# Attention values in seven products with sums of x's quarters, the second head pair's score steps seven slots later, and four branch gates ahead of their gate products

## The chip, the cores and the metric

The kernel runs on one core of one Trainium2 chip. The metric is the device time of one execution in microseconds (us). Before the change the median of three timed runs is 757.07 us (756.86 to 757.54). Engines are named as in the profile: PE is TensorE's matrix multiply, PEld its weight load, DVE is VectorE, ACT is ScalarE, POOL is GpSimd, SP is SyncE, which here only issues DMAs.

## What is computed

One decoder block over 512 tokens of width 1024, in float32. One input projection feeds two token mixers whose outputs are gated, added, projected, normalised, and followed by a feed-forward block. Cut to what matters here:

```python
p = einsum('btd,de->bte', h, w_in) + b_in
a_u, a_v, q, k, v, r, a_low, g_a, g_b = split(p)
y_a = spatial_gating(a_u, a_v, ...)
log_f = log_sigmoid(a_low @ gla_w_gate2 + gla_b_gate) / 16
o = gla_chunked(q, k, v, log_f)          # 4 heads, key 128, value 256
o = o * rsqrt(mean(o**2) + eps)
y_b = o * gla_norm_g * silu(r)
m = sigmoid(g_a) * y_a + sigmoid(g_b) * y_b
h = layer_norm(alpha * h + m @ w_out)
h = layer_norm(alpha * h + square(relu(h @ w_ff1)) @ w_ff2)
```

The change concerns `v` (512 tokens x 1024 values, contracted over 1024), the head pair 1 of `gla_chunked` (heads 2 and 3), and the products `r` and `g_b`.

## The kernel before, in words

**Numbers in two parts.** Every large product is made in three matmul passes. An operand is split into a high part, a rounded copy that ACT writes (CAST, line 88), and a low part, the rest, that DVE writes (TENSOR_TENSOR, line 89). The passes are high x high, high x low and low x high. x lives as `xh`, `xl`; a weight chunk of 128x1024 numbers becomes `wh`, `wl`.

**The weight stream.** `_stream` (line 1109) lists the chunks in order of use. `load_to` issues their DMAs from SP into a ring of three raw buffers, `sum_to` makes sums of chunks where the list asks for them (DVE, line 128), and `split_to` splits them up to seven chunks ahead of PE (`W_BUFS`). A raw buffer is loaded again only when DVE has read it; a `wh`/`wl` buffer is written again only when PE has used it.

**Slots.** PE's order is the order of the program. Each group of 24 matmuls of 128x512 (one bank of PSUM) is a slot; a group is either `row_unit` with tokens as rows (line 218) or `col_job` with tokens as columns (line 691). `at(n, f, phase=...)` puts side work into slot n, and `pump` calls it after that slot's matmuls: first phase MM (other matmuls), then MAIN, then the splits of the next weight chunk, then LATE. DVE, ACT and POOL run in the order in which these calls issue their instructions, strictly one after the other.

**The stages before.** Slots 0 to 7: gating values (`ps`, line 218). 8 to 15: `u`. 16 to 19: q and k of pair 1 (`qk1`). 20 to 27: attention values, two row units of four groups, 8 weight chunks, 192 matmuls; DVE adds the bias row and writes `bufB` (line 785). 28 to 35: `ga`. Then `branch` four times: two slots `r`, two slots `gb`. From 52 on `m @ w_out`, then the feed-forward stage, whose second half already uses seven products for eight (lines 934 to 984, a Strassen-Winograd scheme with three running accumulators).

**Pair 1's score steps.** `plan_pair` (line 589) spreads them: gates (`gates_b`, running sums `cum`), `inter_a`, `inter_e`, `inter_b` (`kd`, `QI`), transposes `pt`, three levels of decayed scores (`level_diff`, `level_prep`, scores `sc`, line 519, masked into `AT` by three DVE copies each, line 532), the diagonal (`diag_a` to `diag_c`, `sd`, line 493), then `chunk_out` (`po`) with the running state `S`. Before, the levels stand in slots 21 to 32, the diagonal's scores in 34 and 35, and `chunk_out` in 36 to 39.

**PSUM.** Eight banks: four for the groups (pool `ps_m`, rotating), two that all score tiles share as one buffer (`ps_s`, tag `sc`, used by `pz`, `sc`, `sd` and by the transposes `yt` in `r_take`, line 797), two of `ps_a`.

**`r_take` and `gb_take`.** After an `r` group PE transposes the attention output into `yt`, ACT makes silu, DVE multiplies (line 801). After a `gb` group ACT makes the sigmoid and DVE multiplies and adds into `AT_` (lines 816, 817); from the second branch on `mh`, `ml` are split at once.

## Time and profile before

| | |
|---|---|
| median of three runs | 757.07 us |
| the profiled execution itself | 757.19 us |
| its span, first to last instruction | 755.4 us |
| PE busy | 746.2 us, 99% of the span |
| DVE busy | 473.8 us, 63% |
| ACT busy | 343.6 us, 45% |
| POOL busy | 29.8 us, 4% |
| DMA moved | 85.14 MB, mean 113 GB/s |
| granted TensorE clock, mean | 0.998 |

The time of an execution is 1.8 us more than its span. A row of the timeline shows start, duration, engine, line, operation, output and inputs; brackets hold the idle time before it and what ended it. A matmul's listed duration (389 ns) overlaps its neighbours; what one costs is the distance between starts.

The same stretch in slices (busy us of each engine) shows DVE at 5.51 of 11 us in the last two `qk1` groups (150 to 161 us) and 8.65 of 11 us in the first two value groups (161 to 172 us).

### The profile page before, as it was taken

How to read it: one execution, taken by the hardware profiler on the slowest of the kernel's cores; microseconds unless marked ns; L12 is line 12 of the kernel's file. 1: busy time of each engine (PE TensorE's matmuls, PEld its weight loads, DVE VectorE, ACT ScalarE, POOL GpSimd, SP SyncE). 2: the span in 40 equal slices, each digit the busy share in tenths (PEclk: the TensorE clock that was granted, in tenths of full speed). 3: DMA queues.
4: the chain of work that ended last, by engine and by line, in shares of the span. 5: the costliest groups of instructions: out<-in, count | busy, mean ns of one | idle time of the engine just before them, and what ended most of it. 6: DMA issues, size and time to landing. Idle time of an engine off the chain costs nothing.

```text
span 755.4 us, 8781 instructions
## 1 busy us (share of the span) xinstructions
PE 746.2 (99%) x3498; PEld 626.0 (83%) x3498; DVE 473.8 (63%) x592; ACT 343.6 (45%) x449; POOL 29.8 (4%) x60
## 2 busy tenths in 40 slices
PE   9999999999999999999999999999999999999996
PEld 7878888888888888888888988888888888888885
DVE  7478876676575554435458533777667856687655
ACT  7375744363254735444222544444444554455300
POOL 1000000000000102000002000000000000000001
PEclk9999999999999999999999999999999999999999
DMA  8533322222042132432240324145331734135111
GB/s 341 203 134 125 132 82 80 84 84 84 31 145 77 56 126 84 170 109 85 98 152 31 109 72 147 49 134 201 111 112 34 244 100 152 56 125 196 43 56 56
DMA packets 25464, 85.14 MB, mean 113 GB/s; under 512 B 3088, under 2 KB 3344, under 8 KB 25424
## 3 DMA queue, kind: packets, MB, share of 16 engines
q1 hardware_dynamic: 25280, 84.33, 32.3%
q8 instruction: 27, 0.44, 0.2%
q10 hardware_dynamic: 144, 0.26, 0.1%
q14 instruction: 13, 0.11, 0.0%
HBM read 82.48 MB, written 2.10 MB: 112 GB/s over the span
## 4 chain that ended last, share of the span: by engine, by line
PE 96%; issue 1%; DVE 1%; DMA 1%; POOL 0%; DVEq 0%; POOLq 0%
PE f L691 22%; PE ps L218 17%; PE mx L974 9%; PE f L1074 6%; PE gb L691 6%; PE r L691 6%; PE ga L691 6%; PE u L691 6%; PE mv L974 4%; PE qk L691 3%; PE first L275 3%; PE m L974 2%; PE sc L519 2%; PE pm L744 1%; PE po L553 1%
## 5 line engine op out<-in xcount | busy, mean ns | idle before, releaser
L89 DVE TENSOR_TENSOR wl<-raw,wh 128x1024 fp32r<-128x1024 f32 x141 | 171.1, 1222 | 114.4 <-ACT wh L88 112.6
L88 ACT CAST wh<-raw 128x1024 fp32r<-128x1024 f32 x141 | 145.7, 1044 | 48.7 <-PE ps L218 23.7
L691 PE MATMUL f<-xh,wh 128*128 128x512 f32 (+1 forms) x288 | 105.4, 366 | 0.0
L691 PE MATMUL f<-xl,wh 128*128 128x512 f32 (+1 forms) x288 | 105.3, 365 | 0.0
L691 PE MATMUL f<-xh,wl 128*128 128x512 f32 (+1 forms) x288 | 105.2, 365 | 0.0
L691 PEld LDWEIGHTS f<-xl,wh 128*128 128x128 f32 x288 | 54.3, 189 | 8.8
L691 PEld LDWEIGHTS f<-xh,wl 128*128 128x128 f32 x288 | 54.3, 189 | 8.7
L691 PEld LDWEIGHTS f<-xh,wh 128*128 128x128 f32 x288 | 54.3, 189 | 8.7
L914 ACT ACTIVATE F<-f 128x512 f32<-128x512 f32 (+1 forms) x28 | 15.0, 537 | 80.2 <-PE f L691 79.1
L218 PE MATMUL ps<-wh,xh 128*128 128x512 f32 x128 | 50.4, 394 | 0.0
L218 PE MATMUL ps<-wh,xl 128*128 128x512 f32 x128 | 49.8, 389 | 0.0
L218 PE MATMUL ps<-wl,xh 128*128 128x512 f32 x128 | 49.8, 389 | 0.0
L974 PE MATMUL mx<-wh,oh 128*128 128x512 f32 x96 | 37.3, 389 | 0.0
L974 PE MATMUL mx<-wl,oh 128*128 128x512 f32 x96 | 37.3, 389 | 0.0
L974 PE MATMUL mx<-wh,ol 128*128 128x512 f32 x96 | 37.3, 389 | 0.0
L128 DVE TENSOR_TENSOR raw<-raw,raw 128x1024 f32<-128x1024 f32 x24 | 29.2, 1218 | 2.6 <-DMA raw<-in_w_all 2.6
L218 PEld LDWEIGHTS ps<-wh,xl 128*128 128x128 f32 x128 | 24.0, 188 | 5.0
L218 PEld LDWEIGHTS ps<-wl,xh 128*128 128x128 f32 x128 | 24.0, 188 | 4.9
L218 PEld LDWEIGHTS ps<-wh,xh 128*128 128x128 f32 x128 | 24.0, 188 | 4.8
L691 PE MATMUL u<-xh,wh 128*128 128x512 f32 x64 | 25.9, 405 | 0.0
L691 PE MATMUL ga<-xh,wh 128*128 128x512 f32 x64 | 25.9, 404 | 0.0
L88 ACT CAST oh<-d 128x1024 fp32r<-128x1024 f32 x12 | 12.6, 1051 | 29.1 <-DVE d L947 29.1
(242 smaller groups left out, 1557.4 us busy)
## 6 DMA issues: line engine op xcount, KB each, us to landing
raw<-in_w_all SPq DMA_DIRECT2D x136, 512.0 KB, 3.4
bufB<-in_head SPq DMA_DIRECT2D x4, 512.0 KB, 8.0
xr<-in_x SPq DMA_DIRECT2D x8, 256.0 KB, 3.5
out<-bufA SPq DMA_DIRECT2D x8, 256.0 KB, 2.0
bufA<-in_head SPq DMA_DIRECT2D x3, 512.0 KB, 5.6
brow<-in_b_in SPq DMA_DIRECT2D x4, 256.0 KB, 6.2
g<-in_ln_g SPq DMA_DIRECT2D x2, 512.0 KB, 5.9
b<-in_ln_b SPq DMA_DIRECT2D x2, 512.0 KB, 5.5
```

What stands on the lines that cost most here:

```text
L88: nc.scalar.copy(hi, src)
L89: nc.vector.tensor_tensor(lo, src, hi.bitcast(F32), op=ALU.subtract)
L128: nc.vector.tensor_tensor(raw, x_, y_, op=ALU.subtract)
L218: nc.tensor.matmul(ps, s_, m_, start=(k == 0 and i == 0), stop=(k == KT - 1 and i == 2))
L275: nc.tensor.matmul(first[e], s_, m_[:, k, :], start=(k == 0 and i == 0), stop=(k == KT - 1 and i == 2))
L519: nc.tensor.matmul(sc[:, c, 0:192], pr.kt[:, jc * P : (jc + 1) * P], pr.qt[:, jc, :], start=True, stop=True)
L553: nc.tensor.matmul(po, pr.AT[:, j, c, :], vs, start=True, stop=(c == 0))
L691: nc.tensor.matmul(ps, s_, m_, start=(k == 0 and i == 0), stop=(k == KT - 1 and i == 2))
L744: nc.tensor.matmul(pm[:, c, :], bufB[:, c, gs], wst[:, g, :], start=True, stop=True)
L914: nc.scalar.activation(dst, ps, AF.Relu)
L974: nc.tensor.matmul(ps, s_, m_, start=(begins and k == 0 and i == 0), stop=(k == 3 and i == 2), skip_group_check=True,)
L1074: nc.tensor.matmul(ps, s_, m_, start=(f == 0 and i == 0), stop=(f == 7 and i == 2))
```

## The change

**Values in seven products.** The values are split in two halves of tokens and columns, and contracted over two halves of 512. x's quarters are summed into four combinations, the weights' quarters into four combinations, and seven products of 24 matmuls each (2 banks of 12) take the place of eight groups. The order is 1, 2, 5, 6, 3, 7, 4. Products 1, 6, 7, 4 run on in one pair of banks, 5 and 3 in another; after each half product DVE adds the bank (running sum included) into a quarter of `bufB`. `value_bank` gives products 2, 5 and 3 the same two banks.

What that takes: 14 weight splits for 8, eight sums of weight chunks on DVE, a second load of x's transposed quarters from `head` into `bufB` (eight DMAs of 256 KB), four sums of quarters (`x_sums`, in slot 19, MAIN), and four splits of the sums (`x_parts`).

**Slots.** The value stage has seven slots (20 to 26). Pair 1's steps move: `gates_b` stays in 18, `inter_a` goes from 19 to 26, the levels from 21..32 to 28..39, the diagonal's scores to 41 and 42, `chunk_out` to 43..46. Thus the levels' later part and the diagonal now stand in the stage of `r` and `gb`.

**Branch order.** `r0 r1 gb0 gb1 r2 r3 gb2 gb3` as before, then `gb4 gb5 gb6 gb7` with their sigmoids kept in `bufB`, then `r4 r5 r6 r7`, each followed by its multiplication, its addition and its split. The four splits of `mh`, `ml` for e below 4 come together before `r4`.

The core of the diff (names and bodies moved without a change left out):

```diff
-    ps_m = pool(ctx, "ps_m", bufs=4, space=PSUM)
+    ps_m = pool(ctx, "ps_m", bufs=1, space=PSUM)
...
+    def bank(name, i=None):
+        if i is None:
+            i = turns[0]
+        turns[0] = (i + 1) % 4
+        return ps_m.tile([P, 512], F32, name=name, tag=f"ps{i}")
...
+    RAW_AT = {(1, 1): (0, 0), (0, 0): (1, 1), (0, 1): (0, 1), (1, 0): (1, 0)}
+    def accumulators(m, name, of):
+        if m in (1, 6, 7, 4):
+            if m == 1:
+                sums["x"] = [of(f"mx{name}_{t}", "x", t) for t in range(2)]
+            return sums["x"], m == 1
+        if m in (5, 3):
+            if m == 5:
+                sums["v"] = [of(f"mv{name}_{t}", "v", t) for t in range(2)]
+            return sums["v"], m == 5
+        return [of(f"m{name}_{t}", "m", t) for t in range(2)], True
...
+    def operands_begin():
+        sgu.close()
+        vgp = pool(vgs, "vgp", side="left")
+        vgp.tile([P, 120], F32, name="pad_v")
+        for (i, j), (a, b) in RAW_AT.items():
+            for k in range(2):
+                k0 = 4 * j + 2 * k
+                nc.sync.dma_start(xq(a, b)[:, k], head[:, k0 : k0 + 2, 256 * i : 256 * i + 256])
+        return vgp
...
-    S_VG, S_GA = 20, 28
-    S_R, S_O = 36, 52
+    S_VG, S_GA = 20, 27
+    S_R, S_O = 35, 51
...
-    plan_pair(pr1, (18, 19, 20, 21), ((21, 23, 24, 25), (25, 27, 28, 29), (29, 30, 31, 32)), 32)
+    plan_pair(pr1, (18, 26, 27, 28), ((28, 30, 31, 32), (32, 34, 35, 36), (36, 37, 38, 39)), 39)
...
+    def x_sums():
+        for o, a, b, op_ in (
+            ((0, 0), (1, 0), (0, 0), ALU.add),
+            ((1, 0), (1, 1), (1, 0), ALU.subtract),
+            ((1, 1), (0, 0), (1, 1), ALU.subtract),
+            ((0, 1), (0, 1), (1, 1), ALU.subtract),
+        ):
+            nc.vector.tensor_tensor(quarter(bufB, *o), quarter(bufB, *a), quarter(bufB, *b), op=op_)
+    at(S_VG - 1, x_sums)
+    at(S_VG - 1, lambda: x_parts(5), phase=LATE)
...
-    for half in range(2):
-        row_unit(xh, xl, copy_take(half, bias_row(C_VG + half * 512)))
+    def value_bank(name, kind, t):
+        return bank(name, (b0 + t + 2 * (kind != "x")) % 4)
+    def value_take(m, t, ps):
+        dst = quarter(bufB, *GOES[m])[:, t, :]
+        nc.vector.tensor_add(dst, brs[GOES[m][1]] if m in NEW else dst, ps)
+    for n, m in enumerate(ORDER):
+        if m == 2:
+            x_parts(6)
+        elif m in (6, 3):
+            x_parts({6: 3, 3: 7}[m])
...
+        product_of(f"v{m}", m, ops, value_take, value_bank, W_BUFS - n // 2)
+        pump(MM, MAIN)
+        pump(LATE)
...
+    for e0 in (0, 2):
         t1 = {e: temp(f"t1_{e}", "brow") for e in (e0, e0 + 1)}
         for e in t1:
             col_job(f"r{e}", r_take(e, t1[e]))
         for e in t1:
-            col_job(f"gb{e}", gb_take(e, t1[e]))
+            col_job(f"gb{e}", gb_take(e, temp(f"gb{e}"), t1[e]))
+    gate = {e: bufB[:, e - 4, 0:512] for e in range(4, KT)}
+    for e in gate:
+        col_job(f"gb{e}", gb_take(e, gate[e]))
...
+        def parts_take(ps, e=e, t1=t1, take=take):
+            take(ps)
+            onto(e, gate[e], t1)
+            split(mh[:, e, :], ml[:, e, :], AT_[:, e, :])
...
+    out += [operand(-1, m, h) for m in ORDER for h in range(2)] + plain(28, n)
```

What moves on the engines shows at three places. First DVE at the end of `qk1` and the start of the values. Before (`wl` are weight splits, `ps_24` the banks of the first value groups):

```order
L381 SCALAR_TENSOR_TENSOR cum1_1297<-ones_97,lf1_1242 128x128 x8
L89 TENSOR_TENSOR wl29_1308<-raw29_1157,wh29_1307 128x1024
L391 TENSOR_TENSOR kd1_1339<-cum1_1297 128x1024
L89 TENSOR_TENSOR wl30_1342<-raw30_1207,wh30_1341 128x1024
L785 TENSOR_TENSOR bufB_92<-ps_24_0_1352,brow_1350 128x512
L401 TENSOR_TENSOR QI1_1268<-QI1_1268,q1_1162 128x1024
```

And DVE of the changed kernel from the row after the running sums on (`raw24<-raw30,raw24` is a sum of weight chunks; `bufB<-bufB` x4 are `x_sums`; `xl5`, `xl6` are splits of x's sums; `mxv1_0` is the first bank of product 1, `mv2_0` that of product 2):

```order
L128 TENSOR_TENSOR raw24_863<-raw30_1162,raw24_863 128x1024
L89 TENSOR_TENSOR wl29_1317<-raw25_865,wh29_1316 128x1024
L857 TENSOR_TENSOR bufB_92<-bufB_92 128x2x512 x4
L128 TENSOR_TENSOR raw25_865<-raw31_1164,raw25_865 128x1024
L89 TENSOR_TENSOR wl30_1354<-raw24_863,wh30_1353 128x1024
L89 TENSOR_TENSOR xl5_1361<-bufB_92,xh5_1360 128x1024
L886 TENSOR_TENSOR bufB_92<-brow_1364,mxv1_0_1368 128x512
L89 TENSOR_TENSOR wl31_1390<-raw25_865,wh31_1389 128x1024
L89 TENSOR_TENSOR wl32_1402<-raw30_1162,wh32_1401 128x1024
L886 TENSOR_TENSOR bufB_92<-brow_1364,mxv1_1_1369 128x512
L89 TENSOR_TENSOR xl6_1407<-bufB_92,xh6_1406 128x1024
L886 TENSOR_TENSOR bufB_92<-bufB_92,mv2_0_1410 128x512
```

Pair 1's `kd` and `QI` are gone from there, and fourteen sums, splits and additions stand between the running sums and the read of product 2's first bank, which is the bank that product 5 takes next.

Second, PE at the end of `r0`. Before:

```order
L691 MATMUL r0_2100<-xh_89,wl40_1763 128x512
L799 MATMUL yt0_2125<-ident_93,bufB_92 128x128 x4
L553 MATMUL po2_0_2132<-bufB_92,AT1_1266 128x256
L557 MATMUL po2_0_2132<-bufB_92,KD1_1269 128x256
L553 MATMUL po3_0_2135<-bufB_92,AT1_1266 128x256
L557 MATMUL po3_0_2135<-bufB_92,KD1_1269 128x256
L691 MATMUL r1_2160<-xh_89,wh41_1809 128x512
```

And in the changed kernel:

```order
L767 MATMUL r0_2083<-xh_89,wh46_1800 128x512
L767 MATMUL r0_2083<-xl_90,wh46_1800 128x512
L767 MATMUL r0_2083<-xh_89,wl46_1801 128x512
L910 MATMUL yt0_2108<-ident_93,bufB_92 128x128 x4
L583 MATMUL sc1_1_0_2115<-qt1_1_1979,kt1_1_2000 128x192 x4
L767 MATMUL r1_2129<-xh_89,wh47_1804 128x512
```

A score tile now follows the transposes at once; both lie in the one buffer `sc`. The same holds after `r1` and `r2`.

Third, DVE around the second head's diagonal. Before (`dr1_1` are its products, `sd1_0` the first head's scores, `dt1_1` the low part that PE's `sd1_1` needs):

```order
L471 TENSOR_TENSOR dr1_1_2005<-q1_1162,k1_1163 128x512
L711 TENSOR_TENSOR bufA_91<-bufA_91,ga5_1976 128x512
L479 TENSOR_TENSOR dr1_1_2005<-dr1_1_2005,q1_1162 128x256
L480 TENSOR_TENSOR dr1_1_2005<-dr1_1_2005,k1_1163 128x256
L89 TENSOR_TENSOR wl45_2048<-raw45_1874,wh45_2047 128x1024
L500 COPY_PREDICATED AT1_1266<-masks_279,sd1_0_2038 128x512
L505 COPY_PREDICATED AT1_1266<-masks_279,sd1_0_2038 128x256
L484 TENSOR_TENSOR dt1_1_2043<-dr1_1_2005,dt1_1_2043 128x768
```

And now:

```order
L535 TENSOR_TENSOR dr1_1_2359<-q1_1169,k1_1170 128x512
L924 TENSOR_TENSOR t1_2_2265<-t1_2_2265,gb2_2362 128x512
L925 TENSOR_TENSOR bufA_91<-bufA_91,t1_2_2265 128x512
L543 TENSOR_TENSOR dr1_1_2359<-dr1_1_2359,q1_1169 128x256
L544 TENSOR_TENSOR dr1_1_2359<-dr1_1_2359,k1_1170 128x256
L89 TENSOR_TENSOR wl59_2401<-raw59_2260,wh59_2400 128x1024
L564 COPY_PREDICATED AT1_1639<-masks_282,sd1_0_2391 128x512
L569 COPY_PREDICATED AT1_1639<-masks_282,sd1_0_2391 128x256
L548 TENSOR_TENSOR dt1_1_2396<-dr1_1_2359,dt1_1_2396 128x768
```

The multiplication with the group `ga5`, which was already a slot old, is replaced by two steps that need the sigmoid of the group `gb2` just made.

## The prediction

> **What bounds the kernel now.** I read the page's head and the summary of its chain first.

> ```profile
> span 755.4 us, 8781 instructions
> PE 746.2 (99%) x3498; PEld 626.0 (83%) x3498; DVE 473.8 (63%) x592; ACT 343.6 (45%) x449; POOL 29.8 (4%) x60
> PE 96%; issue 1%; DVE 1%; DMA 1%; POOL 0%; DVEq 0%; POOLq 0%
> ```

> PE is busy for 99% of the span and carries 96% of the chain. So a matmul less is time less, and every wait that the change puts before a matmul is time more. DVE is at 63% on average, which says nothing about the stage that changes. There I need rows in order of time; the chain, merged, shows PE from the last `qk1` groups to the end of the values.

> ```profile
> 150.31 10.90 PE qk L691 x48
> 161.21 10.88 PE ps L218 x48
> 172.10 0.87 PE pt L408 x8
> 172.97 16.34 PE ps L218 x72
> 189.31 1.30 PE sc L519 x8
> 190.61 5.45 PE ps L218 x24
> 196.06 1.30 PE sc L519 x8
> 197.36 10.89 PE ps L218 x48
> ```

> The reader is to see no gap: PE goes from 150.31 to 208.25 without a wait. A matmul of 128x512 costs 10.88 / 48 = 0.227 us, a slot of 24 costs 5.44 us, a half product of 12 costs 2.72 us.

> **Term 1: matmuls removed.** The values take 7 x 24 = 168 matmuls for 192. 24 x 0.227 = **-5.44 us**. All were on the path. The `pt` and `sc` rows between them (0.87 + 1.30 + 1.30) are moved, not removed.

> **Term 2: PE waits for DVE inside the values.** Product 5 takes the two banks of product 2, directly after it, so its first matmul waits until DVE has added product 2's first bank (`mv2_0`). When DVE gets there is a sum over its queue. Its rows of before:

> ```profile
> 158.31 1.23 DVE L89 TENSOR_TENSOR wl<-raw,wh 128x1024 fp32r<-128x1024 f32 x1 [3.55 <-ACT wh L88]
> 159.45 1.22 DVE L377 TENSOR_TENSOR lf<-lf,ab 128x1024 f32<-128x1024 f32 x1
> 160.71 2.63 DVE L381 TENSOR_TENSOR_SCAN cum<-ones,lf 128x128 f32<-128x128 f32 x8
> 163.25 1.20 DVE L89 TENSOR_TENSOR wl<-raw,wh 128x1024 fp32r<-128x1024 f32 x1
> 164.37 1.22 DVE L391 TENSOR_TENSOR kd<-cum 128x1024 f32<-128x1024 f32 x1
> 165.51 1.22 DVE L89 TENSOR_TENSOR wl<-raw,wh 128x1024 fp32r<-128x1024 f32 x1
> 166.69 0.69 DVE L785 TENSOR_TENSOR bufB<-ps,brow 128x512 f32<-128x512 f32 x1
> 167.30 1.22 DVE L401 TENSOR_TENSOR QI<-QI,q 128x1024 f32<-128x1024 f32 x1
> ```

> DVE starts at 158.31 because ACT's `wh` came only then (its bracket says so), behind pair 1's gates, which don't move. From there one 1024-wide instruction follows the other at 1.14 us (164.37 to 165.51), a 512-wide addition takes 0.61 (166.69 to 167.30). The added chunk sums in slots 16 and 17 fit into the 3.55 us of idle time and I cost them at nothing. The mean of one (the second number after the bar) is from the groups by shape:

> ```profile
> L128 DVE TENSOR_TENSOR raw<-raw,raw 128x1024 f32<-128x1024 f32 x24 | 29.2, 1218 | 2.6 <-DMA raw<-in_w_all 2.6
> L816 DVE TENSOR_TENSOR gb<-gb,t 128x512 f32<-128x512 f32 x8 | 5.5, 692 | 25.0 <-ACT gb L815 25.0
> ```
> ```profile
> L88 ACT CAST wh<-raw 128x1024 fp32r<-128x1024 f32 x141 | 145.7, 1044 | 48.7 <-PE ps L218 23.7 <-DMA raw<-in_w_all 11.0 <-PE mx L974 9.9
> ```

> `x_sums` are the same operation as line 128 on as many numbers, so 1.22 each, 1.14 in a row.

> From the end of the scans at 163.25 the changed queue holds ahead of `mv2_0`: a chunk sum, `wl29`, four `x_sums`, a chunk sum, `wl30`, `xl5`, `wl31`, `wl32`, `xl6`, which is 12 x 1.14 = 13.7 us, and two additions, 1.2 us. So `mv2_0` starts at 178.15 and ends at 178.85. ACT's casts keep ahead: 1.04 us each, one for each of DVE's splits and none for its sums. PE, starting the values at 161.21, is through products 1 and 2 at 161.21 + 48 x 0.227 = 172.1. **PE waits 6.8 us.**

> The second half of product 5 waits for `mv2_1`. Ahead of that stand two chunk sums and two splits: 4 x 1.14 + 0.6 + 0.7, so it ends at 184.05. PE, on again at 178.9, is through the first half at 181.6: **2.4 us more.** After that DVE has per product of 5.44 us at most three or four 1024-wide instructions and two additions, 4.6 to 5.8 us; adding the queue up row by row, products 6, 3, 7 and 4 find their operands about 2 us early or more (the closest: product 4's first bank, free at 201.1, wanted at 203.1). Sum of term 2: **+9.2 us.** The values end at 161.2 + 38.1 + 9.2 = 208.5, with the 3.5 us of `pt` and `sc` still to come.

> How sure is 9.2? If every 1024-wide instruction took 1.1, the first wait is 0.5 smaller. If x's second load came late, it grows: eight loads of 256 KB, most of them released when `mix` has read `bufB` at about 150 us, are needed at 165.5. Loads of that size (the last number is the median to landing):

> ```profile
> xr<-in_x SPq DMA_DIRECT2D x8, 256.0 KB, 3.5
> ```

> So I cost them at nothing. Bounds for term 2: 8.2 to 11.

> **Term 3: transposes and scores share one buffer.** In slots 35, 36 and 39, a score tile stands right behind the transposes `yt` of the same group and needs their buffer. It waits until DVE's multiplication has read `yt`, which waits for ACT's silu. How long that takes, three views of before show for `r0`: the chain, ACT's and DVE's rows.

> ```profile
> 273.28 0.44 PE yt L799 x4
> ```
> ```profile
> 273.32 0.69 ACT L800 ACTIVATE t<-r,cols_sb 128x512 f32<-128x512 f32 x1 [3.83 <-PE r L691]
> ```
> ```profile
> 274.04 0.75 DVE L801 SCALAR_TENSOR_TENSOR t<-yt,cols_sb,t 128x512 f32<-128x512 f32 x1 [2.67 <-ACT t L800]
> ```

> Transposes done at 273.72, buffer free at 274.79 plus about 0.05: 1.1 us. Before, `po` followed there, which lies elsewhere. Three times: **+3.3 us**. It can't be hidden, since nothing stands between on PE. Bounds: 2.5 (0.85 each, if ACT and PE overlap better) to 4.5 (DVE is late once).

> **Term 4: the second head's diagonal.** `sd1_1` needs DVE's low part `dt1_1` and the buffer of `sd1_0`. Before, this was already the one place here where PE waited:

> ```profile
> 253.12 0.43 PE po L553 x2
> ...
> 260.36 0.70 PE sd L493 x4
> 261.06 5.47 PE ga L691 x24
> ...
> 266.57 0.47 DVE dt L484
> ```
> ```profile
> 259.93 1.28 ACT L710 ACT_TABLE_LOAD   x1
> 261.22 0.69 ACT L710 ACTIVATE ga<-ga,cols_sb 128x512 f32<-128x512 f32 x1
> 261.81 0.82 ACT L481 CAST dt<-dr 128x768 fp32r<-128x768 f32 x1
> ```
> ```profile
> 265.52 0.73 DVE L505 COPY_PREDICATED AT<-masks,sd 128x256 f32<-128x256 uint32 x1
> 266.05 0.98 DVE L484 TENSOR_TENSOR dt<-dr,dt 128x768 fp32r<-128x768 f32 x1
> ```

> From the end of the group at 260.36, ACT's sigmoid came 0.86 late (behind the table load), and `dt` ended at 267.03, 6.67 us after the group; the next group and `sd` took 6.2, and PE waited 0.57 us. Two things lengthen it now. The slot before is 5.88 us (0.44 + 5.44) where it was 7.24 (253.12 to 260.36, with four `po` pairs in it), while ACT's and DVE's chain through it stays about 8.1 us (253.12 to 261.22): the sigmoid comes 2.2 late, 1.3 more. And between that sigmoid and the cast of `dt` DVE now has a multiplication and an addition (1.4 us, line 816's 692 ns twice) and the two 256-wide products, which stood ahead of it before (between half of 0.69 and 0.69 each; I take 0.45, 0.9 us): 2.3 more. So `dt1_1` ends 6.67 + 1.3 + 2.3 = 10.3 us after the group, PE is there after about 6.4, and waits 3.9 where it waited 0.57: **+3.3 us**. The other scores of the stage lose at most 0.2 us each, **+0.3 us** together. Bounds: -0.6 (the wait goes altogether) to 4.5.

> **Nothing else.** The `gb` groups ahead of `r`: their order costs no matmul. At the end the chain from `r7` is silu, three DVE steps, cast and split, 0.69 + 0.75 + 0.69 + 0.69, a cast of half the 1.04 us width (at most 1.04) and 0.69 = 4.6 us, and the last part of `mh` is needed 0.44 + 21 x 0.227 = 5.2 us after `r7`: hidden, by a margin of 0.6 us. SP's loads of the next chunks have one slot per chunk after the values.

> **Sum.** -5.44 + 9.2 + 3.3 + 3.3 + 0.3 = +10.7. On the profiled execution's 757.19 us (span 755.4, 1.8 around it, 0.1 above the median): **767.8 us.**

> **The clock.** PE's granted clock falls when PE is idle; the slices at the end show it.

> ```profile
> 748.00:749.00 1.00, 0.41 (x4) 0.20 (x2) 0.52 (x2) 0.00 (x0) 0.00 (x0) 1.00 0.00 0
> 751.00:752.00 1.00, 0.00 (x0) 0.00 (x0) 1.00 (x3) 0.00 (x0) 0.00 (x0) 1.00 0.00 0
> 752.00:753.00 1.00, 0.00 (x0) 0.00 (x0) 0.43 (x1) 0.00 (x0) 0.00 (x0) 0.68 0.36 143
> ```

> The last matmul ends at 748.4, and the clock (third last column) is halved at about 752.4, 4.0 us later. A wait of 6.8 us therefore ends at half clock, one of 3.9 may. At half clock a half product takes 5.44 for 2.72 us. After the first wait that lies within the 2.4 us of the second one, all but 0.3.

> [...]

> **The rivals.**
> [...]
> - *The values alone.* DVE's mean load of 63% leaves room behind the values; if term 4 doesn't come and the buffer waits are short, -5.44 + 9.2 + 2.5 - 0.6: **762.9**. Against it: the order of the rows that term 4 adds up.
> - *Faster.* If the read of product 2's bank is not behind the sums, or DVE is ahead by more than I count, no wait stays and the 24 matmuls and the old wait of 0.57 go: **751.2**. It is decided by whether DVE gets from `wl28` to the end of `mv2_0` in 13.8 us (158.3 to 172.1); my sum is 20.5. For it: DVE's idle time of 3.55 us just before, and a mean load of 63%. Against: that idle time is a wait for ACT which stays.
> - *No change.* The first wait alone, the others hidden: -5.44 + 6.8 - 0.6, **758.0**. Against it: what follows it on DVE, four instructions of 1.14 us in a half product of 2.72.

> **How the numbers follow.** Forecast 0.58; clock on top 0.14; values alone 0.15; faster 0.08; no change 0.05. Slower by over 0.2% (1.5 us, about what a measurement can tell from no change) 0.87, within 0.05, faster 0.08. The range runs from 760.5 (term 2 at 8.2 and terms 3 and 4 at their low ends give 761.9; 1.4 less if the second wait of term 2 is more than halved) to 772 (the clock's upper end).

> **What the changed profile would show.** Right: PE idle before the first matmul of the fifth value bank, put down to DVE's addition, near 6.8 us, and a shorter one of 2 to 2.5 at the next bank; three waits near 1.1 us of `sc` for the multiplication with `yt`; one of 3 to 4 us at `sd`; a clock below 1.00 near 179 us. Wrong: no wait in the values, or waits for DMA there (x's second load), or DVE idle between `cum` and `mv2_0`.

## The result, and the profile after

| | before | after |
|---|---|---|
| median | 757.15 us (756.86 to 757.54, 5 runs) | 772.98 us (772.60 to 774.44, 5 runs) |
| the profiled execution | 757.19 us | 773.63 us |
| its span | 755.4 us | 771.9 us |
| granted TensorE clock, mean | 0.998 | 0.988 |

The ratio is 1.0211 (95% interval 1.0200 to 1.0222): slower, as forecast, and 1.0 us above the range's upper end. One of the four executions of `three`, below, took 1527.99 us, twice as long as its others, for a reason that nothing on record shows; its median here is that of the other three. The head of the page after, and the shares of its chain:

```profile
PE 747.3 (97%) x3474; PEld 624.6 (81%) x3474; DVE 502.9 (65%) x620; ACT 352.1 (46%) x458; POOL 29.9 (4%) x60
PE 88%; DVE 6%; ACT 3%; issue 2%; DMA 1%; POOL 0%; DVEq 0%; ACTq 0%; POOLq 0%
```

PE has 24 matmuls less and yet 1.1 us more busy time, since some of them ran at half clock. Its share of the chain fell from 96% to 88%; DVE, which had 1%, has 6%: PE now waits for it. What PE waits for between 150 and 400 us (in total, times, longest):

```profile
PE mvv L372 <- DVE bufB L886: 7.6, 2, 7.4
PE sd L557 <- DVE AT L569: 4.4, 1, 4.4
PE sc L583 <- DVE t L912: 3.4, 3, 1.1
```

`mvv` are the two banks of products 5 and 3, `AT` the masked scores, `t` the product with `yt`. These are the three places that the prediction named. To see what they cost, take PE's timeline at three borders: the first matmul of the values (161.05 before, 161.00 after), of `ga0`, and of the stage after the last branch. The two borders of before, and of after:

```profile
208.09 0.39 PE L691 MATMUL ga<-xh,wh 128*128 128x512 f32 x1
...
367.32 0.39 PE L218 MATMUL ps<-wh,mh 128*128 128x512 f32 x1
```
```profile
209.18 0.39 PE L767 MATMUL ga<-xh,wh 128*128 128x512 f32 x1
...
383.05 0.48 PE L227 MATMUL ps<-wh,mh 128*128 128x512 f32 x1
```

At the last border the change is 15.7 us behind. From there to the last matmul (748.4 before, 764.7 after) another 0.6 us comes in small pieces, in which the profile shows no wait of PE. The values took 48.2 us instead of 47.0, although 3.5 us of `pt` and `sc` have left them. Like for like they cost 4.7 us more; the other 11 us arise between the borders, in the stage of `r` and `gb` (the `ga` stage before it runs without a wait).

The clock also shows in the windows (stretch, its length, busy time of PE, PEld, DVE, ACT, POOL, then the granted clock third from the end):

```profile
176.00:177.00 1.00, 0.00 (x0) 0.00 (x0) 1.00 (x2) 0.00 (x0) 0.00 (x0) 0.89 0.00 0
183.00:184.00 1.00, 1.00 (x5) 0.77 (x3) 1.00 (x2) 0.00 (x0) 0.00 (x0) 0.70 0.32 94
...
323.00:324.00 1.00, 0.00 (x0) 0.00 (x0) 0.89 (x1) 1.00 (x3) 0.00 (x0) 0.77 0.00 0
330.00:331.00 1.00, 1.00 (x5) 0.77 (x5) 0.37 (x1) 0.00 (x0) 0.00 (x0) 0.81 0.75 213
```

A clock of 0.5 for a part of a slice gives the moment: it halves at 176.78, is back at 183.60, halves at 323.54 and is back at 330.38. The second half-speed stretch hits `sd1_1` and `gb4`, with nothing to hide it.

### The profile page after: what moved, and what is told of

Its sections match the earlier page's. It is cut to its first block, busy times and chain, and to the rows that moved or that the text cites. A ratio compares the mean times of both kernels' runs of the same rounds, so it can differ in the third digit from the quotient of the medians.

```text
span 771.9 us, 8815 instructions
## 1 busy us (share of the span) xinstructions
PE 747.3 (97%) x3474; PEld 624.6 (81%) x3474; DVE 502.9 (65%) x620; ACT 352.1 (46%) x458; POOL 29.9 (4%) x60
## 4 chain that ended last, share of the span: by engine, by line
PE 88%; DVE 6%; ACT 3%; issue 2%; DMA 1%; POOL 0%; DVEq 0%; ACTq 0%; POOLq 0%
PE f L767 22%; PE ps L227 11%; PE mx L372 8%; PE r L767 6%; PE ga L767 6%; PE u L767 6%; PE f L1154 5%; PE gb L767 4%; PE mv L372 4%; PE first L286 3%; PE sc L583 2%; PE m L372 2%; PE mxv L372 2%; DVE wl L89 2%; PE qk L767 1%
## 5 line engine op out<-in xcount | busy, mean ns | idle before, releaser
L89 DVE TENSOR_TENSOR wl<-raw,wh 128x1024 fp32r<-128x1024 f32 x147 | 178.1, 1222 | 123.8 <-ACT wh L88 122.6
L88 ACT CAST wh<-raw 128x1024 fp32r<-128x1024 f32 x147 | 151.6, 1044 | 62.6 <-DVE raw L128 19.1
L128 DVE TENSOR_TENSOR raw<-raw,raw 128x1024 f32<-128x1024 f32 x32 | 39.0, 1218 | 2.6 <-DMA raw<-in_w_all 2.5
L767 PE MATMUL gb<-xh,wh 128*128 128x512 f32 x64 | 26.3, 412 | 0.0
L88 ACT CAST oh<-d 128x1024 fp32r<-128x1024 f32 x12 | 12.6, 1051 | 29.1 <-DVE d L1057 29.1
L767 PE MATMUL r<-xh,wh 128*128 128x512 f32 x64 | 25.8, 404 | 0.0
L767 PE MATMUL gb<-xh,wl 128*128 128x512 f32 x64 | 25.5, 399 | 0.0
L767 PE MATMUL gb<-xl,wh 128*128 128x512 f32 x64 | 25.4, 397 | 0.0
L227 PE MATMUL ps<-wh,mh 128*128 128x512 f32 x64 | 25.2, 393 | 0.0
L227 PE MATMUL ps<-wh,xh 128*128 128x512 f32 x64 | 25.2, 393 | 0.0
## 6 DMA issues: line engine op xcount, KB each, us to landing
bufB<-in_head SPq DMA_DIRECT2D x8, 256.0 KB, 4.3
xr<-in_x SPq DMA_DIRECT2D x8, 256.0 KB, 3.8
out<-bufA SPq DMA_DIRECT2D x8, 256.0 KB, 2.0
brow<-in_b_in SPq DMA_DIRECT2D x4, 256.0 KB, 6.5
```

What stands on the lines that cost most here:

```text
L88: nc.scalar.copy(hi, src)
L89: nc.vector.tensor_tensor(lo, src, hi.bitcast(F32), op=ALU.subtract)
L128: nc.vector.tensor_tensor(raw, x_, y_, op=ALU.subtract)
L227: nc.tensor.matmul(ps, s_, m_, start=(k == 0 and i == 0), stop=(k == KT - 1 and i == 2))
L767: nc.tensor.matmul(ps, s_, m_, start=(k == 0 and i == 0), stop=(k == KT - 1 and i == 2))
```

## The experiments

All kernels are the change with the edit shown; times are medians of timed runs, beside 757.1 to 757.2 for before on the same chips.

### What holds the values back

**own_banks**: product 2 away from product 5's banks.

```diff
     def value_bank(name, kind, t):
+        if kind == "m":
+            return ps_a.tile([P, 512], F32, name=name, tag="aux")
```

> Product 2 gets two PSUM banks of its own (the free pair of ps_a), so product 5 no longer waits for product 2's additions. Theory 'DVE queue' (DVE's work in the values is longer than PE's, the bank only shows it): PE starts product 5 at about 174 us, after a wait of about 2 us instead of 7.4, but stands again for about 5 us before product 3, whose x parts DVE still ends near 190 us; gain 2.5 us at most, about 770.5 us, less if that second wait halves the clock. Rival 'shared bank' (the wait comes from the buffer alone): the 7.4 us wait shrinks to about 2 and nothing takes its place, 5.5 us faster, about 767.5 us.

Measured: 772.12 us (ratio 1.0195, 1.0180 to 1.0210), 0.9 faster. PE's waits of this kernel in the values:

```profile
PE mvv L372 <- DVE xl L89: 4.6, 2, 3.2
PE mvv L372 <- DVE bufB L888: 0.6, 1, 0.6
```

The wait of 7.4 us is gone and 5.2 us have come in its place, 3.2 of them before product 3 and followed by half clock (0.50 from 189 to 190 us). The shared bank was where the wait showed, not what it was made of: DVE's queue sets the pace.

**pool_sums**: the sums of x's quarters on the idle engine.

```diff
-            nc.vector.tensor_tensor(quarter(bufB, *o), ...)
+            nc.gpsimd.tensor_tensor(quarter(bufB, *o), ...)
```

> The four sums of x's quarters (5.0 us on DVE) go to POOL, which is idle there; nothing else changes. Theory 'DVE queue': everything behind them on DVE comes 5 us earlier, so PE's wait before product 5 falls from 7.4 to about 2.4 us, the next one stays near 2.3, and the clock stays at 1.00 there: about 5 us faster, 768 us. Rival: POOL takes longer for the sums than DVE, or slows DVE beside it, and the x parts come as late as before: no gain, 772 to 774 us. (No row of the trace has such a sum on POOL.)

Measured: 773.42 us (1.0210, 1.0193 to 1.0227), no gain. One sum on POOL and two instructions of DVE beside it:

```profile
160.96 3.26 POOL L857 TENSOR_TENSOR bufB<-bufB 128x1024 f32<-128x1024 f32 x1
```
```profile
158.56 3.40 DVE L89 TENSOR_TENSOR wl<-raw,wh 128x1024 fp32r<-128x1024 f32 x1 [2.41 <-ACT wh L88]
161.88 3.41 DVE L441 TENSOR_TENSOR lf<-lf,ab 128x1024 f32<-128x1024 f32 x1
```

In the change, with POOL idle there, these two instructions take 1.23 and 1.22 us; beside POOL's sums they take 3.40 and 3.41: 2 x 2.2 us lost there, of the 5.0 that left the queue.

**no_sums**: the same load taken off DVE without giving it to POOL.

```diff
-    at(S_VG - 1, x_sums)
```

> Leaves out the four sums of x's quarters (the products take the quarters as they are), so that DVE has 5.0 us less ahead of product 5 and POOL nothing more. Theory 'DVE queue': PE's wait before product 5 falls from 7.4 to about 2.4, the next is about 2.3, the clock stays at 1.00: 5 us faster than the change, 768 us. Rival: something else than DVE's work holds the bank (x's load, ACT): 772 us or more.

Measured: 769.89 us (1.0168, 1.0152 to 1.0184), 3.1 faster; the waits are 2.6 and 2.2 us, as expected. The values took 45.0 us for 48.2. The rest of the 5 us went to the clock, which fell at 180.41, behind the two waits, for one stretch of 3.41 us with nothing to hide it. What DVE has queued, and not x's load or ACT, makes the first wait.

**three**, **three_pool**, **three_no_sums**, **three_no_dve**: `own_banks`, `own_yt` and `late_onto` (both below) together, then with the sums on POOL, left out, and with the sums of weight quarters left out too.

```diff
-                if less:
+                if less and i > 40:
```

> own_banks, own_yt and late_onto together. Theory 'separate terms': their gains add up, 0.9 + 2.2 + 3.7 = 6.8 us, 766.2 us; the waits of the scores for the rows yt and the fall of the clock at sd1_1 go, the waits of product 5 and product 3 for x's parts stay. Rival: the waits share DVE's queue, and what one frees is late at the next: 768 us or more.

> The same three, and the sums of x's quarters on POOL. Theory 'DVE queue': the 5 us that leave DVE take away the waits of 1.4, 0.6 and 3.2 us for x's parts and the half clock behind the last of them: about 6 us below 'three', near 760 us, and still slower than before. Rival: POOL is late with the sums: like 'three', 766 us.

> 'three' without the four sums of x's quarters. Theory 'DVE queue': product 3's x parts come 5 us earlier, near 185 us, PE waits about 2.5 us there instead of 1.4 + 0.6 + 3.2 in three places: 4 to 6 us below 'three', about 761 us. Rival: as 'three', 766 us.

> 'three' without the four sums of x's quarters and without the eight sums of weight quarters (the products take quarters as they are; 14 us less on DVE). Theory: no wait stays in the values, which end about 8.5 us earlier than in 'three': about 758 us. So even with DVE's added work taken out, the 5.4 us of fewer matmuls are about eaten by what the displaced score steps still cost. Rival: the values still wait for loads or ACT: 762 us or more.

Measured: 766.03 (1.0115, 1.0099 to 1.0132), 765.76 (1.0118, 1.0099 to 1.0137), 759.53 (1.0029, 1.0019 to 1.0039) and 758.14 us (1.0015, 1.0005 to 1.0024). The gains of the three add up (7.0 us for 6.8). POOL helps no more here than alone: that expectation was 6 us off, as it left out that the two DVE instructions take 3.40 and 3.41 us beside POOL's sums here too. Without the sums of x's quarters 6.5 us go, a little more than the 4 to 6 expected: the values take 40.0 us for 46.4, since the waits shrink from 5.2 to 1.3 us and no half clock follows them (189 to 190 us at 1.00, in `three` at 0.50). In the profiled execution (758.25 us) the clock didn't fall at `sd1_1` either. That is not so in most: of nine executions three took 757.9 to 758.3 us at a mean clock of 0.997, and six 759.5 to 760.6 at 0.994 or 0.995. Without any sums no wait is left in the values, as the waits of `three_no_dve` between 150 and 400 us show, all of them:

```profile
PE sd L557 <- DVE AT L569: 2.0, 1, 2.0
PE sc L583 <- DVE kt L528: 1.3, 1, 1.3
```

Its `ga0` starts 38.1 us after the values, which is seven times 5.44. Yet it isn't faster than before: the 5.44 us are eaten by what the displaced score steps still cost (6.3 us in `shift_fixed` below). No version that computes the whole reference came below before.

### The buffer of `yt`

**own_yt**

```diff
-            pt = ps_s.tile([P, 2, NCH, P], F32, name=f"yt{e}", tag="sc")[:, 0]
+            if e < 4:
+                pt = ps_a.tile([P, NCH, P], F32, name=f"yt{e}", tag="aux")
+            else:
...
```

> The transposed rows yt of r0 to r3 go to the free pair of ps_a instead of the one buffer of the scores. Theory (term 3 of the prediction): the three waits of 1.1 us of sc for the multiplication with yt go and nothing else changes, 3.3 us faster, about 769.7 us. Rival: the scores' preparation on DVE and ACT is late anyway, so the same scores wait for that instead, under 1 us faster, about 772.5 us.

Measured: 770.74 us (1.0177, 1.0162 to 1.0192), 2.2 faster. The three waits go, and one new one comes, for the preparation of the third level:

```profile
291.68 1.54 PE L583 MATMUL sc<-qt,kt 128*128 128x192 f32 x8 [1.26 <-DVE kt L528]
```

From `r0` to `r1` it is 7.05 us here and 8.44 in the change, so one such place cost 1.4 us, not the 1.1 that the wait shows: a wait is counted from the modelled end of the transposes, 0.60 us after their start, and where nothing waits what follows starts 0.43 us after it (`yt` 290.40 and `sc` 290.83 in `three_no_sums`).

### The diagonal

**late_onto**: `gb2`'s multiplication and addition go behind the diagonal's steps.

```diff
-            if t1 is not None:
+            if e == 2:
+                at(slot[0], lambda: onto(e, gate, t1), phase=LATE)
+            elif t1 is not None:
...
```

> The multiplication and addition (1.4 us) of gb2's gate move on DVE behind the copies of sd1_0 and the low part of sd1_1's operand. Theory (term 4): PE's wait at sd1_1 falls from 4.4 to about 3.0 us. If the clock falls only after 4.0 us of idle time, as the prediction had it, it then stays at 1.00 and sd1_1 (1.92 us) and gb4 (6.77 us) go back to about 0.7 and 5.45: 3.9 us faster in all, 769.1 us. Rival 'grid' (the clock is decided at the ends of fixed stretches of 3.41 us, one of which ends at 323.55 us whatever the wait's length): it falls at 323.55 us all the same, 1.4 us faster, 771.6 us, or up to 2 us more if it comes back one stretch earlier. Rival 'ACT': the sigmoid behind the table load sets the time, no gain.

Measured: 769.30 us (1.0161, 1.0146 to 1.0176), 3.7 faster. The wait fell by 2.4 us to 2.0, not by 1.4: the two 256-wide products (0.9 us) stood behind the same sigmoid and came free with it. In the profiled execution the clock didn't fall there (matmuls of 128x512 start 0.23 us apart behind it, from 324.6 on). The total fits the 4.0 us that the prediction took, but other runs with the same wait of 2.0 us (`three`, `three_pool`, `shift_fixed`, `three_no_dve`) did show the fall (in `three` matmuls start 0.43 us apart from 320.7 to 323.7).

**early_copies**, **early_both**: first `sd1_0`'s copies, then also the low part `dt1_1` ahead of the weight split.

```diff
-        at(n, take, phase=LATE)
+        at(n, take, phase=MAIN if pr.hp and not j else LATE)
...
-        at(diag + 2, lambda: diag_c(pr, 1), phase=LATE)
+        at(diag + 2, lambda: diag_c(pr, 1), phase=MAIN if pr.hp else LATE)
```

> The two masked copies of sd1_0 stand on DVE ahead of the diagonal's products and the weight split instead of behind them. Theory (the prediction's term 4: the low part dt1_1, behind the cast and the weight split, is what comes last, near 326.5 us): the wait put down to the copies shrinks by about 2 us, but one of the same length for dt1_1 takes its place; no change, 773 us. Rival: the copies behind the split are the cause: 2 us faster or more with the clock, 769 to 771 us.

> As early_copies, and the low part dt1_1 ahead of the weight split. Theory: sd1_1 gets its last operand about 2 us earlier: 2 us faster, 771 us, and up to 1.7 us more if the clock's half stretch shrinks from two stretches of 3.41 us to one. Rival: ACT's sigmoid and cast set the time: no gain.

Measured: 773.88 us (1.0216, 1.0201 to 1.0232) and 771.17 us (1.0180, 1.0161 to 1.0198). PE's timeline of `early_copies`:

```profile
323.88 0.49 PE L557 MATMUL sd<-dt,ones_r 128*128 128x512 f32 x1 [2.05 <-ACT dt L545]
326.96 1.22 PE L557 MATMUL sd<-dt,ones_r 128*128 128x512 f32 x3 [2.58 <-DVE dt L548]
```

Both theories held (`early_copies` lies within the change's own range). The change's profile blames the copies (`AT`), but with them out of the way PE stands just as long for the cast and the low part of `dt1_1`: removing the releaser that a wait names shows only the next one.

### The clock by itself

**fill**, **fill_all**: matmuls whose result nobody reads, in PE's waits.

```diff
+        for i in range(n):
+            nc.tensor.matmul(ps, ones_r, xh[:, 0, :], start=True, stop=True)
...
```

> Adds matmuls whose result is not used in two of PE's waits: 24 (5.4 us) ahead of product 5 and 12 (2.7 us) ahead of sd1_1. They keep PE busy, so that the clock should stay at 1.00, and end before what PE waits for. Theory: at sd1_1 the clock costs 2.5 us on top (1.92 against 0.7, 6.77 against 5.45), which goes; in the values the half clock of product 5's first half was hidden by the wait for the next bank, so that nothing is won there: 2.5 us faster in all, about 770.5 us. Rival: the clock's cost lies on top in both places, 4.7 us faster, 768.3 us. Rival: the clock costs nothing that the waits don't hide, no change.

> Matmuls whose result is not used fill nearly all of PE's three waits: 30 ahead of product 5, 10 ahead of its second half, 18 ahead of sd1_1. Theory 'grid' (the clock halves at the end of a fixed stretch of 3.41 us in which PE was busy for less than about half): no stretch is now that idle, the clock stays at 1.00 up to the end of the kernel's matmuls, sd1_1 and gb4 take about 1.4 and 5.5 us, nothing is won in the values: about 2 us faster than the change, 771 us. Rival: the clock's fall is hidden behind the waits: 773 us.

Measured: 774.62 us (1.0224, 1.0207 to 1.0241), 1.6 slower, and 771.39 us (1.0189, 1.0171 to 1.0207), 1.6 faster. `fill` was expected at 770.5 us, 2.5 faster, and came out slower. The first matmuls of product 5's two halves in it, and two of its windows:

```profile
179.58 0.47 PE L372 MATMUL mvv<-wh,xh 128*128 128x512 f32 x1 [1.75 <-DVE bufB L892]
184.75 0.50 PE L372 MATMUL mvv<-wh,xh 128*128 128x512 f32 x1 [2.16 <-DVE bufB L892]
```
```profile
185.00:186.00 1.00, 1.00 (x5) 0.77 (x5) 1.00 (x2) 0.00 (x0) 0.00 (x0) 0.80 0.57 229
189.00:190.00 1.00, 1.00 (x6) 0.83 (x5) 0.98 (x2) 0.79 (x1) 0.00 (x0) 1.00 0.10 37
```

The filler kept the clock through the first wait, but the wait of 2.2 us that follows brought it down, at 185.60, 0.85 us *after* PE was at work again. The rest of product 5 ran at half speed with no wait behind it to hide that, and the values took 1.6 us longer (49.8 for 48.2). At `sd1_1` its 12 matmuls left a wait of 1.6 us, and the clock fell all the same, at 328.95: `gb4` took 6.85 us, 6.81 in the change, so the gain forecast there didn't come. With all three waits filled (`fill_all`) the clock stays at 1.00 up to the last matmuls, the values take as long as in the change (48.2), and the way from `ga0` to the last border is 1.8 us shorter (172.1 for 173.9). So in the change the first fall is hidden and the second costs **1.8 us**.

### The displaced score steps without the values

**shift_alone**: the values as two row units again; pair 1's steps and the gates as late as in the change, one slot more since the values take eight.

```diff
-    for n, m in enumerate(ORDER):
-        product_of(f"v{m}", m, ops, value_take, value_bank, W_BUFS - n // 2)
+    for half in range(2):
+        row_unit(xh, xl, copy_take(half, bias_row(C_VG + half * 512)))
...
-    plan_pair(pr1, (18, 26, 27, 28), ((28, 30, 31, 32), (32, 34, 35, 36), (36, 37, 38, 39)), 39)
+    plan_pair(pr1, (18, 27, 28, 29), ((29, 31, 32, 33), (33, 35, 36, 37), (37, 38, 39, 40)), 40)
```

> The values are computed as before (two row units, eight slots); the second pair's score steps come as late as in the change (one slot more, since the values take eight), and the gates gb4 to gb7 stand ahead of r4 to r7. Theory (terms 3 and 4 and the clock do not depend on the values): three waits of 1.1 us, a wait of 4.4 instead of 0.57 us at sd1_1 and 2.5 us for the half clock behind it: +9.7 us, 766.9 us; the clock's part can be up to 1 us off, as it depends on when the wait falls. Rival: the wait at sd1_1 is DVE's backlog from the values: it comes back to under 1 us, 757 + 3.4, about 761 us.

Measured: 769.03 us (1.0156, 1.0141 to 1.0172), 11.8 slower than before and 2.1 more than expected (0.8 is what the three places of `yt` cost beyond their waits of 1.13 us, 3 x 0.26, 0.4 stands in `sd1_0`, which takes 1.1 us instead of 0.7; the rest is spread). Its borders, from a first matmul at 161.08:

```profile
204.60 0.39 PE L752 MATMUL ga<-xh,wh 128*128 128x512 f32 x1
...
378.26 0.48 PE L227 MATMUL ps<-wh,mh 128*128 128x512 f32 x1
```

The values take 43.5 us here, 48.2 in the change: the seven products by themselves cost 4.7 us. From `ga0` to the last border it is 173.7 us here, 173.9 in the change and 159.2 before, plus the 3.5 us that moved in: the displacement costs 11 us, with or without the seven products. That the order of the gates alone costs nothing wasn't tried by itself: `r4` to `r7` need pair 1's output, which now comes only with slot 46.

**shift_fixed**: the same with `own_yt` and `late_onto`.

> shift_alone with own_yt and late_onto: the values as before, the displaced score steps with a buffer of their own for yt and gb2's two DVE steps moved back. Theory: their gains are those that they have beside the seven products, 2.2 + 3.7 us: 763.1 us, 6 us above before. Rival: without the values' load on DVE more comes back: 760 us or less.

Measured: 763.49 us (1.0077, 1.0062 to 1.0092), as expected: 5.5 of the 11.8 us come back.

## Why the prediction was right and wrong

The sign, the three places and the mechanism of the waits held. What failed is the clock behind the wait at `sd1_1`, which the sum put at nothing; terms 2 to 4 came out too small as well. The sizes add up so (us; measured between the borders of the traces, the clock's from `fill_all`):

| term | predicted | measured | how measured |
|---|---|---|---|
| 1, 24 matmuls less | -5.4 | -5.4 | `three_no_dve`: values in 38.1 |
| 2, waits in the values | +9.2 | +10.1 | 48.2 - 43.5 + 5.4 |
| 3, `yt` and scores in one buffer | +3.3 | +4.2 | 3 x (8.44 - 7.05) |
| 4, the wait at `sd1_1` | +3.3 | +4.5 | `gb3` to the end of `gb4`, 18.55 for 12.22 at the same place before (`ga7`, `sd1_1`, `r0`), less the clock |
| clock behind it | 0 | +1.8 | `fill_all` |
| the rest | +0.3 | +0.5 | what remains, 0.4 of it in `sd1_0` |
| sum | +10.7 | +15.7 | 383.05 - 367.32 |

**Term 1** held, and can be seen only where DVE is relieved of the sums.

**Term 2** held in its working. DVE's rows of the change:

```profile
163.20 1.20 DVE L128 TENSOR_TENSOR raw<-raw,raw 128x1024 f32<-128x1024 f32 x1
164.32 1.22 DVE L89 TENSOR_TENSOR wl<-raw,wh 128x1024 fp32r<-128x1024 f32 x1
165.45 4.99 DVE L857 TENSOR_TENSOR bufB<-bufB 128x1024 f32<-128x1024 f32 x4
...
178.57 0.68 DVE L886 TENSOR_TENSOR bufB<-bufB,mv 128x512 f32<-128x512 f32 x1
```

The scans end at 163.2 as before, and `mv2_0` begins at 178.57 where 178.15 was worked out; most of the difference is the four `x_sums`, which take 1.23 apiece in a row (165.45 to 170.37) instead of 1.14. PE's rows at product 5:

```profile
179.39 0.77 PE L372 MATMUL mvv<-wh,xh 128*128 128x512 f32 x1 [7.36 <-DVE bufB L886]
...
184.56 0.50 PE L372 MATMUL mvv<-wh,xh 128*128 128x512 f32 x1 [0.23 <-DVE bufB L886]
```

7.4 for 6.8 us; the second wait shrank to 0.2 because half-speed matmuls filled it, which the paragraph on the clock had said. The 10.1 us are 7.6 of waits and 2.5 of half speed. The values ended at 209.2, forecast 208.5. What term 2 didn't say is that the bank is exchangeable: `own_banks` shows the same loss at the next operand.

**Term 3** took the wait for its price. The three waits are 1.13 us each as worked out, but each place costs 1.39 (8.44 - 7.05), 0.26 more.

**Term 4** is the wait that was mis-sized most. The chain was right: sigmoid, two DVE steps, two products, cast, low part. The rows of the change, PE and DVE:

```profile
325.87 1.92 PE L557 MATMUL sd<-dt,ones_r 128*128 128x512 f32 x4 [4.42 <-DVE AT L569]
```
```profile
323.11 1.23 DVE L89 TENSOR_TENSOR wl<-raw,wh 128x1024 fp32r<-128x1024 f32 x1 [1.84 <-ACT wh L88]
324.25 0.72 DVE L564 COPY_PREDICATED AT<-masks,sd 128x512 f32<-128x512 uint32 x1
325.00 0.72 DVE L569 COPY_PREDICATED AT<-masks,sd 128x256 f32<-128x256 uint32 x1
325.53 0.98 DVE L548 TENSOR_TENSOR dt<-dr,dt 128x768 fp32r<-128x768 f32 x1
```

`dt1_1` ends at 326.5, 0.8 us behind the copies that the wait is put down to, so the term named the last operand rightly (`early_copies` confirms it). But it comes 11.6 us after the end of `gb2`'s group (314.9), and 10.3 were worked out. The whole difference lies in "ACT's and DVE's chain through it stays about 8.1 us": from the end of the group before (`r3`, 308.96) to the sigmoid it is 9.4. ACT's rows, first of before, where that group ended at 253.12, then of the change:

```profile
253.93 0.83 ACT L481 CAST dt<-dr 128x768 fp32r<-128x768 f32 x1
...
256.60 1.28 ACT L474 ACT_TABLE_LOAD   x1
258.74 0.44 ACT L474 ACTIVATE dr<-lf 128x256 f32<-128x256 f32 x1 [0.86 <-DVE dt L484]
```
```profile
309.00 0.69 ACT L911 ACTIVATE t<-r,cols_sb 128x512 f32<-128x512 f32 x1 [3.73 <-PE r L767]
311.30 0.83 ACT L545 CAST dt<-dr 128x768 fp32r<-128x768 f32 x1 [1.61 <-DVE dr L544]
...
315.29 1.28 ACT L538 ACT_TABLE_LOAD   x1 [2.20 <-DVE dt L548]
...
318.33 0.69 ACT L929 ACTIVATE gb<-gb,cols_sb 128x512 f32<-128x512 f32 x1
```

The cast of the first head's operand came 0.8 us after its group and now comes 2.3 after it: `r3`'s silu and DVE's multiplication with `yt` (0.69 and 0.75) stand ahead of the products that it waits for, where nothing but a `ga` addition of a slot ago stood before. Of these 1.5 us 0.7 are left at the end of `dt1_0`, as two squares of `po` (0.9 us on ACT) no longer follow the cast. The table load ahead of the exponential, which before ran while ACT had to wait anyway, now comes after that wait (1.3 us more; why it does, the rows don't show), and two scalings of `po` (0.8 us) are gone. In sum the sigmoid comes 1.3 us later. The working moved the chain to its new slots and didn't ask what its new neighbours put in front.

**The clock** is the step that failed. The text took from one fall that the clock halves 4.0 us after PE's last matmul, and so left the wait of 3.9 us at `sd1_1` at full speed ("one of 3.9 may"); the clock on top had a chance of 0.14. The wait became 4.4 us, but the clock fell 2.1 us after PE stopped (321.45 to 323.54) and cost 1.8 us. The range's upper end, 772, leaves about 4 us above the forecast to the clock, an allowance that no run shows; the runs showed 6.82 us of half speed at the first wait, hidden, and 6.84 us at the second, at 1.8 us. With the clock held (`fill_all`) the kernel takes 771.39 us, inside the range. Terms 2, 3 and 4 came out within the bounds that they were given (up to 11, 4.5 and 4.5), but all on the upper side; these errors were not put on top of the clock, and so the range ended 1.0 us short. The clock's first fall is hidden, as the prediction had it.

## What to carry to other kernels

Fewer matmuls pay only where the engine that prepares their operands has room in *that stage*: here 5.4 us of PE were bought with 14 us of sums (4 x 1.23 + 8 x 1.14) and ten more splits of 1.14 us on a queue that was busy for 8.65 of 11 us there before, and its mean load of 63% said nothing about that. When work is moved to make room, add up the chain at the place where it lands: the displaced score steps cost 11 us, twice the whole saving. And when a wait names a buffer, ask what stands in the queue ahead of it before giving it another buffer.

## What the runs showed of the hardware

**The spread grew.** Before, with no such wait, the runs range over 0.7 us (756.86 to 757.54), the change's over 1.8 (772.60 to 774.44), the size of one fall's cost. The two groups of `three_no_sums` lie about as far apart. That the grid's place makes the difference fits, but wasn't shown.
